# One list schedule for the layer norm, projections, short convolutions and preparation of a hybrid DeltaNet and mixture-of-experts layer

## The chip, the cores and the metric

The kernel runs on one core of one Trainium2 chip. The metric is device time in microseconds (us), the median of several runs. The engines are TensorE (PE, matrix products), VectorE (DVE), ScalarE (ACT), GpSimd (POOL) and SyncE (SP), whose queue issues most of the transfers (DMA).

## What is computed

One layer over 1024 latent tokens and 256 context tokens, width 1024. One input projection feeds a gated DeltaNet of four heads and a Conformer convolution; their outputs go through one output projection, and a mixture of 64 experts follows. The changed stage computes the parts in this excerpt that stand before the chunked scan: the Conformer's layer norm, the projections, the 7-tap convolutions, norms and decays, and the triangular matrix of each chunk with the inverse of its 16x16 diagonal blocks.

```python
u = modulate(rmsnorm(x, g_mix), sh1, sc1) @ w_in           # the same for ctx; columns: q k v | z | ba | cf
qkv = silu(depthwise_conv_seq(qkv, conv_w))                # 7 taps, ctx and x are separate sequences
q, k = l2norm(q) * DN_DK ** -0.5, l2norm(k)
beta, g = sigmoid(ba[0]), -exp(a_log) * softplus(ba[1] + dt_bias)
gc = cumsum(g)                                             # inside a chunk
decay = exp(gc[:, None] - gc[None, :])
lmat = strict_lower((k * beta) @ k.T * decay)
tinv = triangular_solve(eye + lmat, eye)                   # then the scan over the chunks
y = silu(layernorm(dwconv(cf[:512] * sigmoid(cf[512:])) + dw_b, ln_g, ln_b))
x = x + gt1 * (concat(gated_head_norm(o, z), y) @ w_out)
x = x + gt2 * moe_ffn(modulate(rmsnorm(x, g_ffn), sh2, sc2))
return rmsnorm(x, g_final)
```

## The kernel before

Feature maps lie with channels on the partitions and tokens along the row. `hTh` and `hTl` are the high and low part of the modulated input, 1280 tokens (256 of context first). A projection block is 128 output columns: `load_w` (L302 to L305) loads the weights in two halves into `wst`, ACT copies the high part `whi`, and POOL subtracts for the low part `wlo` (`split`, L293 and L294); `fm` (L320) makes three products for each of 8 slices of the depth (`hTh` and `hTl` by `whi`, `hTh` by `wlo`), for a context segment of 256 columns and two latent segments of 512.

The stage begins behind the Conformer's 31 taps on DVE (L427). Its pieces:

- the layer norm of `ycv`, two halves of 512 tokens: channel mean on PE (L462, L466), subtraction, squares, variance, `Sqrt`, reciprocal, `Silu`, store to `hc_d` (L462 to L488);
- twelve `qkv_block`s, four each for k, v and q: projection, copy into `cx` (latent) and `cc` (context) with zero edges, `conv7` (first tap on ACT, six on DVE, L548), `Silu` (L569). Blocks of k and v are then transposed on PE (L573), scaled and stored to `kv_d`; `key_norms` follows the k blocks;
- four `z_block`s: projection, `Silu`, store;
- `prep1` for five pairs of chunks (L694 to L717): the factors `rr` (L694), the key products (L698), the running sums of `gg` (L701, products of `rr` and a triangle), their `Exp` in `dm` (L703), factors `nb` (L706, L707), and the matrix `wt` (L708), which is stored to `wt_d`. Its diagonal blocks are gathered into `bounce` (L714) and spread over all partitions into `rep`, 1 MB (L717);
- `base_inverse` for each pair: 15 elimination steps on DVE (`tm` L730, `xf` L731), which read `rep`;
- `conv_out` for two column halves, eight row tiles each: the Conformer's part of the output projection from `hc_d` and the residual `x` (`hx`, L602 to L614);
- the query norms (`sqq` L766, L767, L772) and their scale `ssq` (L775). Then the next stage begins on DVE with `yy` (L846).

In this stage the program text gives the work piece by piece, and an automatic scheduler sets the order on each engine; `first()` puts the splits at high priority. From L793 on (`manual_schedule`) the order is written out: the class `Order` takes operations, each with an engine, a duration, the keys that it reads and writes, and a latency (0.2 unless given) before its result can be used, simulates them, and emits them by the longest path that is left. The later stages (inverses, scan, routing, experts) are such lists.

Of the kernel before, what the change touches and what calls it, by code (L numbers as in the profile page):

```python
# [149 lines left out]
def hybrid_kernel(tc, a, out):  # L150
# [318 lines left out]
    for hf in range(2):
        sl = slice(hf * 512, (hf + 1) * 512)  # L470
        pm = channel_mean(lambda j: ycv[:, j, sl])
        for j in range(4):
            V.tensor_sub(ycv[:, j, sl], ycv[:, j, sl], pm)

        def square(j):
            sq = lnp.tile([128, 512], F32, name="sql", bufs=2)
            S.activation(sq, ycv[:, j, sl], AF.Square)
            return sq

        pv = channel_mean(square)  # L480
        rv = lnp.tile([128, 512], F32, name="rv", bufs=1)
        V.tensor_scalar(rv, pv, EPS, None, op0=OP.add)
        S.activation(rv, rv, AF.Sqrt)
        V.reciprocal(rv, rv)
        for j in range(4):
            V.tensor_mul(ycv[:, j, sl], ycv[:, j, sl], rv)
            S.activation(ycv[:, j, sl], ycv[:, j, sl], AF.Silu, scale=vcol('ln_g', j), bias=vcol('ln_b', j))
            SY.dma_start(hc_d[:, j, sl], ycv[:, j, sl])  # L488
# [11 lines left out]
    def sct(name):  # L500
        return keep.tile([128, 2, 10, 4], F32, name=name)

    beta, gg = sct("beta"), sct("gg")
    tmp = lnp.tile([128, 2, 10, 4], F32, name="tmp")
    S.activation(beta, bav[:, 0], AF.Sigmoid)

    def per_dh(t):
        return t.rearrange("p (d h) -> p d h", d=2)[:, :, None, :].to_broadcast([128, 2, 10, 4])

    V.tensor_tensor(gg, bav[:, 1], per_dh(alb[:, 1]), op=OP.add)  # L510
    S.activation(tmp, gg, AF.Abs)
    S.activation(tmp, tmp, AF.Exp, scale=-1.0)
    S.activation(alb[:, 0], alb[:, 0], AF.Exp)
# [36 lines left out]
    def qkv_block(blk):  # L550
# [1304 lines left out]
```

## Time and profile before

| what | value |
|---|---|
| median of 3 runs | 1735.74 us (1734.1 to 1737.79) |
| the profiled execution | 1735.59 us, span 1733.9 us |
| mean granted clock of PE over the span | 0.968 |
| PE busy in the span | 1593.5 us (92%) |
| DVE | 992.9 us (57%) |
| ACT | 494.5 us (29%) |
| POOL | 534.4 us (31%) |

"Busy" is the time in which an engine runs an instruction; the share is of the whole span, in which the experts' products fill the second half. The changed stage lies between about 212 and 563 us. "Granted clock" is the share of full speed that PE was allowed; the two levels are 2.4 GHz (1.00) and 1.2 GHz (0.50). In the rows, `<-` behind a tile names what it is made from, and behind an idle time what ended it.

### The profile page before, as it was taken

What the parts mean: (1) busy time and instruction counts of PE and PEld (TensorE: products, weight loads), DVE (VectorE), ACT (ScalarE), POOL (GpSimd) and SP (SyncE); (2) the same over time, 40 slices, a digit from 0 to 9 for tenths busy, and PEclk for the clock granted to TensorE, in tenths of its full rate; (3) what the DMA queues carried; (4) which work ended last, traced back from release to release, by engine and by line L of the source; (5) the groups of instructions that cost most, each with busy time, mean ns of one, the idle gap of its engine ahead of it and who ended that gap; (6) DMA issues with size and microseconds to landing.
All of it is one profiled execution on the core that took longest, in us unless ns stands there. A gap on an engine that the chain in (4) does not pass through costs nothing. (4 is left out here: it accounts for less than half of the span.)

```text
span 1733.9 us, 23484 instructions
## 1 busy us (share of the span) xinstructions
PE 1593.5 (92%) x8380; PEld 933.8 (54%) x8380; DVE 992.9 (57%) x2236; ACT 494.5 (29%) x1072; POOL 534.4 (31%) x487
## 2 busy tenths in 40 slices
PE   5989999877759999798999999999999999999995
PEld 1557667765537899787544433444444344443442
DVE  2588988889671886877712443434344434343424
ACT  4541266634122212444212121212121211111212
POOL 1321214543212777832011232323232323232310
PEclk9999999997979999899999999999999999999997
DMA  9455123444643334766358999999999999999957
GB/s 312 160 174 178 38 65 95 111 113 123 169 141 123 121 104 150 242 217 219 119 218 305 338 335 332 314 364 314 323 383 361 329 330 322 324 385 347 353 131 246
DMA packets 151114, 404.35 MB, mean 233 GB/s; under 512 B 21175, under 2 KB 68692, under 8 KB 125396
## 3 DMA queue, kind: packets, MB, share of 16 engines
q1 hardware_dynamic: 131146, 338.82, 53.9%
q0 software_dynamic: 18288, 59.26, 14.5%
q10 hardware_dynamic: 1562, 4.76, 0.7%
q8 instruction: 67, 1.10, 0.3%
q14 instruction: 51, 0.42, 0.1%
HBM read 339.48 MB, written 71.43 MB: 237 GB/s over the span
## 5 line engine op out<-in xcount | busy, mean ns | idle before, releaser
L1353 PE MATMUL gu<-wg,hg 128*32 128x512 f32 (+2 forms) x1968 | 463.2, 599 | 0.6 <-issue 0.6
L1632 DVE SCALAR_TENSOR_TENSOR ob<-dn,wc,gt2b 128x512 f32<-128x512 f32 x124 | 93.1, 750 | 366.0 <-PE dn L1373 366.0
L1641 POOL DMA_INDIRECT acc<-ob,ic x89 | 134.6, 1512 | 527.5 <-DVE st L1563 467.1
L1353 PEld LDWEIGHTS gu<-wg,hg 128*32 128x32 f32 (+2 forms) x1968 | 148.4, 137 | 203.1 <-issue 159.2
L1373 PE MATMUL dn<-wd,sg 128*32 128x512 f32 (+2 forms) x984 | 226.8, 597 | 0.5 <-ACT sg L1364 0.5
L1607 ACT ACTIVATE hg<-xt,mf 128x128 f32<-128x128 f32 x248 | 93.4, 456 | 376.0 <-PE xt L1601 376.0
L320 PE MATMUL a<-hTh,whi 128*128 128x512 f32 (+1 forms) x448 | 172.0, 384 | 5.2 <-ACT cx L557 2.8
L320 PE MATMUL a<-hTl,whi 128*128 128x512 f32 (+1 forms) x448 | 170.3, 380 | 0.0
L320 PE MATMUL a<-hTh,wlo 128*128 128x512 f32 (+1 forms) x448 | 169.5, 378 | 0.0
L1373 PEld LDWEIGHTS dn<-wd,sg 128*32 128x32 f32 (+2 forms) x984 | 77.8, 137 | 143.5 <-issue 142.7
L294 POOL TENSOR_TENSOR wlo<-wst,whi 128x512 fp32r<-128x512 f32 x56 | 82.5, 1489 | 220.5 <-ACT whi L293 220.3
L1605 DVE TENSOR_SCALAR hg<-xt,mf 128x128 f32<-128x128 f32 x248 | 84.4, 402 | 50.8 <-PE xt L1601 50.8
L427 DVE SCALAR_TENSOR_TENSOR ycv<-yg,cfw,ycv 128x64 f32<-128x64 f32 (+14 forms) x120 | 101.3, 844 | 6.1 <-ACT ycv L421 2.9
L320 PEld LDWEIGHTS a<-hTh,whi 128*128 128x128 f32 x448 | 85.1, 190 | 32.4 <-issue 13.3
L1591 POOL DMA_INDIRECT xg<-xn_d,ig x62 | 76.7, 1237 | 63.9 <-issue 20.6
L320 PEld LDWEIGHTS a<-hTh,wlo 128*128 128x128 f32 x448 | 85.0, 190 | 18.4 <-issue 3.4
L320 PEld LDWEIGHTS a<-hTl,whi 128*128 128x128 f32 x448 | 85.1, 190 | 17.8 <-issue 3.0
L1552 DVE TENSOR_TENSOR oh<-posl 128x1024 bf16<-128x1024 f32 (+3 forms) x89 | 77.6, 897 | 0.0
L1601 PE MATMUL xt<-ident,xg 128*128 128x128 f32 x496 | 70.3, 285 | 0.0
L293 ACT ACTIVATE whi<-wst 128x512 fp32r<-128x512 f32 x56 | 33.0, 624 | 111.3 <-PE a L320 65.5
L1358 DVE TENSOR_TENSOR sg<-sg,gu 128x256 f32<-128x256 f32 x62 | 26.1, 421 | 63.7 <-ACT sg L1357 63.7
L1357 ACT ACTIVATE sg<-gu 128x256 f32<-128x256 f32 x62 | 23.8, 384 | 135.2 <-PE gu L1353 135.2
(444 smaller groups left out, 2503.7 us busy)
## 6 DMA issues: line engine op xcount, KB each, us to landing
wg<-exp_w_gate SPq DMA_DIRECT2D x64, 1024.0 KB
wg<-exp_w_up SPq DMA_DIRECT2D x64, 1024.0 KB
wd<-exp_w_down SPq DMA_DIRECT2D x64, 1024.0 KB
wm<-w_mod SPq DMA_DIRECT2D x24, 1024.0 KB
wst<-w_in SPq DMA_DIRECT2D x48, 256.0 KB
kv<-kv_d SPq DMA_DIRECT2D x20, 512.0 KB
rep<-bounce SPq DMA_DIRECT2D x5, 1024.0 KB
eb<-egr_d SPq DMA_DIRECT2D x18, 256.0 KB
```

What stands on the lines that cost most here:

```text
L294: eng.tensor_tensor(lo, st, hi.bitcast(F32), op=OP.subtract)
L320: PE.matmul(ps[:, :n], l[:, k, :], r[:, k, t0:t0 + n], start=(k == 0 and i == 0), stop=(k == 7 and i == 2))
L427: V.scalar_tensor_tensor(yc[:, lo:hi], yg[:, lo + d:hi + d], cfw[:, t * 4 + j:t * 4 + j + 1], yc[:, lo:hi], op0=OP.mult, op1=OP.add)
L1353: PE.matmul(pgu[o:o + n, :].rearrange("p (a f) -> p a f", a=2), lhsT(k, o, n), wts[r][0][:, :, k, :], start=(k == 0), stop=(k == 7), tile_ ...
L1373: PE.matmul(pd[o:o + n, :], aT[:, k, o:o + n], wts[r][1][:, k, hf * 512:(hf + 1) * 512], start=(k == 0), stop=(k == 1), tile_position=(0, ...
L1552: V.tensor_tensor(oh[:, :, o:o + n], N.iol[:, None, p0:p0 + n].to_broadcast([128, 8, n]), N.posr[:, :, r:r + 1].to_broadcast([128, 8, n]), ...
L1591: G.indirect_dma_start(out=xg, out_offset=None, in_=xn_d, in_offset=bass.IndirectOffsetOnAxis(ap=ig, axis=0), bounds_check=1023, oob_is_er ...
L1601: PE.transpose(pt[:, csl(q)], nth(B['xg'][:, 0:1024], 4 * j + q, 8), ident)
L1605: V.tensor_scalar(hg[:, k, :], pt[:, csl(q)], sc_[:, k:k + 1], sh_[:, k:k + 1], op0=OP.mult, op1=OP.add)
L1607: S.activation(hg[:, k, :], pt[:, csl(q)], AF.Identity, scale=sc_[:, k:k + 1], bias=sh_[:, k:k + 1])
L1632: V.scalar_tensor_tensor(ob[:, hs_], res[hf], B['wc'], N.gt2b[:, hs_], op0=OP.mult, op1=OP.mult)
L1641: G.indirect_dma_start(out=acc_d[turn[0]], out_offset=bass.IndirectOffsetOnAxis(ap=ic[:n], axis=0), in_=B['ob'][o:o + n], in_offset=None, ...
```

## The change

The whole stage is listed with `Order` and emitted as one list, under `manual_schedule`, which now begins ahead of it, as do the eight PSUM banks `bk` of the later stages. Helpers `TE`, `DVE`, `ACT`, `POOL` and `DMA` add an operation with its duration. The list's lengths are, for example, 2.76 us for half of a 512-column projection segment, 1.7 for a tap over 1283 columns, 0.62 for a high part, 1.35 for a low part, 0.8 for most transfers, and 3.0 with a latency of 4.0 for the spread. A second `Order()` follows for the later stages. With the listing go these edits:

- `kf` and the k and v blocks have 1283 columns: context, three zeros, latent. One `conv7` pass of 1283 replaces two (1024 and 256); `ksl(c)` finds a chunk. The zero edges of `cx` are cleared once.
- `prep1` makes two fp32 factors `rr`, both on POOL, and two fp32 products with `Ls` and `Us` (L869 of the changed kernel), in place of four rounded factors (two on POOL, two on DVE) and four products; the casts `LUr` and `ghl` go.
- The low part of `conv_out`'s `hcr` is always POOL's; it alternated between DVE and POOL.
- After the k blocks there is a third pair of weight tiles; the k blocks have two more output tiles and a second `sq` in `qf`; the spread goes into two halves of `qf` in turn (`rep_of`), in place of a tile `rep`.
- All `z` blocks stand with the v blocks, and `conv_out(0)` ahead of the second half of the q blocks in the list's text.

```diff
-    def conv7(dst, src, blk, n):
-        for t in range(7):
-            wt = cnv[:, t * 12 + blk:t * 12 + blk + 1]
-            if t == 0:
-                S.activation(dst, src[:, 0:n], AF.Copy, scale=wt)
-            else:
-                V.scalar_tensor_tensor(dst, src[:, t:t + n], wt, dst, op0=OP.mult, op1=OP.add)
...
-        for ci, c in enumerate(pair):
-            wt = prp.tile([128, 4, 128], F32, name="wt", bufs=1)
-            rr_ = [prp.tile([128, 4, 128], F32R, name="rr", tag=t, bufs=1) for t in ("rf", "rl", "rb")]
-            rr_.append(cvp.tile([128, 4, 128], F32R, name="rr", tag="sq", bufs=1))
-            for i, t in enumerate(rr_):
-                (G, V, G, V)[i].tensor_tensor(t, bm((Ui, Li)[i // 2]), b3(ghl[i % 2][:, i // 2, c].bitcast(F32)), op=OP.mult)
-            yield
-            kk = bank("b")
-            for h in range(4):
-                PE.matmul(kk[:, csl(h)], kf[:, h, csl(c)], kf[:, h, csl(c)], start=True, stop=True)
-            sg = bank("b")
-            for i, t in enumerate(rr_):
-                PE.matmul(sg, LUr[i // 2], flat(t), start=(i == 0), stop=(i == 3))
-            dm = prp.tile([128, 4, 128], F32, name="dm", bufs=1)
-            S.activation(flat(dm), sg, AF.Exp)
-            nb = prp.tile([128, 4, 128], F32, name="nb", bufs=1)
-            for h in range(4):
-                S.activation(nb[:, h], Ui, AF.Identity, scale=nbd[:, c, h:h + 1], bias=nb2b[:, c, h:h + 1])
-            G.tensor_tensor(nb, nb, dm, op=OP.mult)
-            V.tensor_mul(wt, h4(kk), nb)
...
-        rep = prp.tile([128, 2048], F32, name="rep", bufs=1)
-        SY.dma_start(rep, bass.AP(tensor=bounce.tensor, offset=bounce.offset, ap=[[2048, 8], [0, 16], [1, 2048]]))
...
-    prp = st_cv.enter_context(tc.tile_pool(name="prep", bufs=1, reuse_waits="tile"))
-    key_norms()
-    for h in range(4):
-        run_together([prep1(pairs[h])])
-        qkv_block(8 + h)
-        run_together([base_inverse(pairs[h])])
-    for h in range(3):
-        qkv_block(h)
-        if h == 0:
-            run_together([prep1(pairs[4])])
-        if h == 1:
-            run_together([base_inverse(pairs[4])])
-    run_together([conv_out(0)])
-    qkv_block(3)
-    z_block(0)
-    run_together([conv_out(1)])
-    for h in (1, 2):
...
+    def o_load_w(src, k=8, by=None):
+        j = turn_of("w", N.wbufs)
+        hi, lo = (lambda sl, t=t: t[j].rearrange("p (k n) -> p k n", k=k)[:, sl] for t in (WH, WL))
+        keys = []
+        open_ = ["prep"] if j == 2 else []
+        for i in range(0, k, k // 2):
+            s = turn_of("ws", 3)
+            sl, st, ks_ = slice(i, i + k // 2), WS[s].rearrange("p (k n) -> p k n", k=k // 2), f"ws{s}"
+            kh_, kl_ = f"wh{j}{2 * i // k}", f"wl{j}{2 * i // k}"
+            DMA(0.75, lambda st=st, sl=sl: SY.dma_start(st, src[:, sl, :]), w=[ks_])
+            if by is not None:
+                DVE(0.8, lambda st=st: V.tensor_tensor(st, st, by()[:, None, :].to_broadcast([128, k // 2, 1024 // k]),
+                                                       op=OP.mult), r=["rr3"], w=[ks_])
+            ACT(0.62, lambda st=st, sl=sl: S.activation(hi(sl), st, AF.Copy), r=[ks_, *open_], w=[kh_])
+            POOL(1.35, lambda st=st, sl=sl: G.tensor_tensor(lo(sl), st, hi(sl).bitcast(F32), op=OP.subtract),
+                 r=[ks_, kh_], w=[kl_])
+            keys += [kh_, kl_]
+        return hi, lo, keys
...
+        open_ = ["prep"] if kind == 2 else []
+        ACT(1.4, lambda: tap(0), r=[kc, *open_], w=[kd])
+        for t in range(1, 7):
+            DVE(1.7, lambda t=t: tap(t), r=[kc], w=[kd])
...
+            ACT(0.63, lambda hs=hs, parts=parts: S.activation(parts()[0], hs, AF.Copy), r=[ko], w=[ka])
+            POOL(1.35, lambda hs=hs, parts=parts: G.tensor_tensor(parts()[1], hs, parts()[0].bitcast(F32),
+                                                                  op=OP.subtract), r=[ko], w=[ka])
...
+    def rep_of(n):
+
+        h = 0 if n % 2 else 2
+        return qf[:, h:h + 2, :].rearrange("p a t -> p (a t)"), [f"qf{h}", f"qf{h + 1}"]
+
+    def o_prep1(n):
+        bounce = dp.tile([8, 16, 2, 4, 16], F32, name="bounce", bufs=3)
+        for ci, c in enumerate(pairs[n]):
+            krr = [f"rr{2 * ci + i}" for i in range(2)]
+            for i in range(2):
+                POOL(1.5, lambda i=i, c=c, ci=ci: G.tensor_tensor(
+                    N.RR[2 * ci + i], bm((Ui, Li)[i]), b3(gg[:, i, c]), op=OP.mult), r=["gg", "prep"], w=[krr[i]])
+            b, kb = bbank()
+
+            def products(b=b, c=c):
+                for h in range(4):
+                    PE.matmul(b[:, csl(h)], kf[:, h, ksl(c)], kf[:, h, ksl(c)], start=True, stop=True)
+
+            TE(0.95, products, r=[f"kf{h}" for h in range(4)], w=[kb])
+            b2_, kb2 = bbank()
+
+            def running(b=b2_, ci=ci):
+                for i in range(2):
+                    PE.matmul(b, (Ls, Us)[i], flat(N.RR[2 * ci + i]), start=(i == 0), stop=(i == 1))
+
+            TE(1.8, running, r=krr, w=[kb2])
+            ACT(0.6, lambda b=b2_: S.activation(flat(N.DM), b, AF.Exp), r=[kb2, "prep"], w=["dm"])
+
+            def factors(c=c):
+                for h in range(4):
+                    S.activation(N.NB[:, h], Ui, AF.Identity, scale=nbd[:, c, h:h + 1], bias=nb2b[:, c, h:h + 1])
+
+            ACT(1.9, factors, r=["b2", "prep"], w=["nb"])
+            POOL(1.35, lambda: G.tensor_tensor(N.NB, N.NB, N.DM, op=OP.mult), r=["dm"], w=["nb"])
+            DVE(0.7, lambda b=b: V.tensor_mul(N.WT, h4(b), N.NB), r=[kb, "nb"], w=["wt"])
+            DMA(0.8, lambda c=c: SY.dma_start(wt_d[c], N.WT), r=["wt"], w=[f"wtd{c}"])
+            if c >= 2:
+                DMA(0.8, lambda c=c: SY.dma_start(dm_d[c - 2], N.DM), r=["dm"])
+
+            def gather(ci=ci, c=c):
+                src = wt_d[c]
+                SY.dma_start(bounce[:, :, ci], bass.AP(tensor=src.tensor, offset=src.offset,
+                                                       ap=[[16 * 512 + 16, 8], [512, 16], [128, 4], [1, 16]]))
+
+            DMA(1.0, gather, r=[f"wtd{c}"], w=[f"bn{n}{ci}"])
+
+        def spread():
+            SY.dma_start(rep_of(n)[0], bass.AP(tensor=bounce.tensor, offset=bounce.offset,
+                                               ap=[[2048, 8], [0, 16], [1, 2048]]))
+
+        O("DMA", 3.0, spread, [f"bn{n}0", f"bn{n}1", "prep"], rep_of(n)[1], 0, 4.0)
...
+    def o_base_inverse(n):
+        kr = rep_of(n)[1]
+
+        def steps(m0, m1):
+            rep, xf = rep_of(n)[0], N.xf
+            if m0 == 0:
+                V.tensor_copy(xf.rearrange("p d u c -> p (d u) c"), Ic[:, None, :].to_broadcast([128, 16, 16]))
+            for m in range(m0, m1):
+                k = 15 - m
+                tm = N.tm[m % 2]
+                tgt = view(xf, m + 1, [[128 - (m + 1), 2], [16, 8], [1, k]])
+                src = view(xf, m, [[128 + 15 - 2 * m, 2], [16, 8], [0, k]])
+                wr = view(rep, m * 128 + m + 1, [[(15 - 2 * m) * 128 - (m + 1), 2], [16, 8], [1, k]])
+                V.tensor_tensor(tm[:, :, :, :k], src, wr, op=OP.mult)
+                V.tensor_tensor(tgt, tgt, tm[:, :, :, :k], op=OP.add)
+
+        for m0 in range(0, 15, 3):
+            DVE(2.3, lambda m0=m0: steps(m0, m0 + 3), r=[*kr, "ic"], w=["xf"])
...
+    POOL(0.6, pads, w=["cx0", "cx1"])
+    for hf in range(2):
+        o_norm_half(hf)
+    o_scalars()
+    for h in range(4):
+        o_qkv(4 + h)
+    o_masks()
+    once(open_prep, w=["prep", "rv", "sql0", "sql1", "gs", "egr", *(f"y{j}{hf}" for j in range(4) for hf in range(2))])
+    N.wbufs, turns["w"], turns["ot"] = 3, -1, 0
+    o_key_norms()
+    for h in range(4):
+        o_prep1(h)
+        o_qkv(8 + h)
+        o_z(h)
+        o_base_inverse(h)
+    o_qkv(0)
+    o_prep1(4)
+    o_qkv(1)
+    once(open_out, w=["ac0", "ac1"])
+    o_conv_out(0)
+    o_base_inverse(4)
+    o_qkv(2)
+    o_qkv(3)
+    o_conv_out(1)
+    o_query_norms()
+    O.emit()
```

PE at the start of the stage: `ycv` is the Conformer's result, `gtc` and `ms` belong to the stage before, and the rows `a<-hTh,whi` and so on are projections. Before:

```order
L320 MATMUL a<-hTl,whi 128x512
L320 MATMUL a<-hTh,wlo 128x512
L320 MATMUL a<-hTh,whi 128x512
L438 MATMUL b<-ident,gtc 32x128
L462 MATMUL b<-ycv,ones 32x512 x3
L320 MATMUL a<-hTl,whi 128x512
L320 MATMUL a<-hTh,wlo 128x512
```

Now (`bk_...` are the banks, `rv` the copied mean, L670 the projections):

```order
L256 MATMUL a<-wm,csil 32x512 x7
L265 MATMUL b<-ident,ms 128x128 x4
L438 MATMUL b<-ident,gtc 32x128
L524 MATMUL bk_1381<-ycv,ones 32x512 x4
L528 MATMUL bk_1382<-rv,onm 128x512
L524 MATMUL bk_1381<-ycv,ones 32x512 x3
L670 MATMUL bk_1378<-hTh,whi 128x512
L670 MATMUL bk_1378<-hTl,whi 128x512
```

Before, projections stand ahead of and behind the first products with `ycv`; now these products and the mean's L528 stand ahead of all projections.

DVE at the first base inverse: `ac` are a v block's taps, `wt` is a chunk's matrix, `tm<-xf,rep` the first reader of the spread. Before:

```order
L548 SCALAR_TENSOR_TENSOR ac<-cx,cnv,ac 128x1024
L548 SCALAR_TENSOR_TENSOR ac<-cc,cnv,ac 128x256
L708 TENSOR_TENSOR wt<-b,nb 128x512
L548 SCALAR_TENSOR_TENSOR ac<-cc,cnv,ac 128x256
L694 TENSOR_TENSOR rr<-Ui,gg_1537 128x512
L548 SCALAR_TENSOR_TENSOR ac<-cc,cnv,ac 128x256
L694 TENSOR_TENSOR rr<-Li,gg_1537 128x512
L548 SCALAR_TENSOR_TENSOR ac<-cc,cnv,ac 128x256
L548 SCALAR_TENSOR_TENSOR ac<-cx,cnv,ac 128x1024
L730 TENSOR_TENSOR tm<-xf,rep 128x16x15
```

Now (L719 the taps, L745 the scaling of a transposed v block, L880 `wt`, L913 and L914 the steps; the spread lies in `qf`):

```order
L745 TENSOR_TENSOR ot_1406<-bk_1381,rk 128x256
L719 SCALAR_TENSOR_TENSOR ac_2047<-cx_1404,cnv,ac_2047 128x1283 x6
L906 COPY xf<-Ic 128x256
L913 TENSOR_TENSOR tm_2057<-xf,qf 128x16x15
L914 TENSOR_TENSOR xf<-xf,tm_2057 128x2x8x15
L913 TENSOR_TENSOR tm_2058<-xf,qf 128x16x14
L914 TENSOR_TENSOR xf<-xf,tm_2058 128x2x8x14
L913 TENSOR_TENSOR tm_2057<-xf,qf 128x16x13
L914 TENSOR_TENSOR xf<-xf,tm_2057 128x2x8x13
L880 TENSOR_TENSOR wt<-bk_1382,nb 128x512
```

All six taps of the second v block stand ahead of the first reader of the spread, in one run, and the third `wt` stands behind it and three steps.

DVE at the second base inverse, before:

```order
L548 SCALAR_TENSOR_TENSOR ac<-cx,cnv,ac 128x1024
L736 TENSOR_TENSOR yc<-yc,Ic 128x128
L723 COPY xf<-Ic 128x256
L548 SCALAR_TENSOR_TENSOR ac<-cx,cnv,ac 128x1024
L548 SCALAR_TENSOR_TENSOR ac<-cc,cnv,ac 128x256
L694 TENSOR_TENSOR rr<-Ui,gg_1537 128x512
L730 TENSOR_TENSOR tm<-xf,rep 128x16x15
L548 SCALAR_TENSOR_TENSOR ac<-cc,cnv,ac 128x256
L731 TENSOR_TENSOR xf<-xf,tm 128x2x8x15
L708 TENSOR_TENSOR wt<-b,nb 128x512
```

Now:

```order
L745 TENSOR_TENSOR ot_1405<-bk_1384,rk 128x256
L719 SCALAR_TENSOR_TENSOR ac_2046<-cx_1403,cnv,ac_2046 128x1283 x2
L906 COPY xf<-Ic 128x256
L913 TENSOR_TENSOR tm_2057<-xf,qf 128x16x15
L914 TENSOR_TENSOR xf<-xf,tm_2057 128x2x8x15
L913 TENSOR_TENSOR tm_2058<-xf,qf 128x16x14
L914 TENSOR_TENSOR xf<-xf,tm_2058 128x2x8x14
L913 TENSOR_TENSOR tm_2057<-xf,qf 128x16x13
L914 TENSOR_TENSOR xf<-xf,tm_2057 128x2x8x13
L719 SCALAR_TENSOR_TENSOR ac_2046<-cx_1403,cnv,ac_2046 128x1283
```

Two of the six taps of the third v block stand ahead of the reader of the spread, and the next one behind three steps.

## Rows read from the trace of the kernel before

**Rows 1.** Windows: us; busy (x count) of PE, PEld, DVE, ACT, POOL; PEclk; DMA.

```profile
187.00:212.00 25.00, 23.50 (x125) 17.44 (x123) 24.00 (x34) 2.24 (x4) 6.29 (x16) 1.00 0.13 32
212.00:563.00 351.00, 290.26 (x1292) 220.58 (x1293) 259.70 (x429) 153.09 (x245) 109.44 (x105) 0.91 0.41 116
```

**Rows 2.** Timeline of PE at the start of the stage.

```profile
212.19 1.04 PE L462 MATMUL b<-ycv,ones 128*32 128x512 f32 x2 [1.70 <-DVE ycv L427]
```

**Rows 3.** Timeline of DVE at the end of the stage.

```profile
562.09 0.17 DVE L773 COPY ssq<-b 128x16 f32<-128x16 f32 x1 [6.13 <-PE b L772]
563.25 1.29 DVE L846 TENSOR_TENSOR yy<-yc,bd 128x512 f32<-128x512 f32 x2
```

**Rows 4.** Waits of 212 to 563: us in total, times, longest.

```profile
DVE tm L730 <- DMA rep<-bounce: 23.6, 5, 9.5
DVE hx L613 <- DMA hx<-x: 16.4, 4, 5.1
```

**Rows 5.** Timeline of SP's DMA queue and of DVE: start, us.

```profile
326.42 0.64 SPq L717 DMA_DIRECT2D rep<-bounce  x1
338.40 0.41 DVE L730 TENSOR_TENSOR tm<-xf,rep 128x240 f32<-128x240 f32 x1 [1.25 <-DMA rep<-bounce]
428.54 0.60 SPq L717 DMA_DIRECT2D rep<-bounce  x1
442.01 0.41 DVE L730 TENSOR_TENSOR tm<-xf,rep 128x240 f32<-128x240 f32 x1 [4.09 <-DMA rep<-bounce]
```

**Rows 6.** Timeline of PE, two pieces: start, us, records.

```profile
285.48 0.40 PE L320 MATMUL a<-hTh,whi 128*128 128x512 f32 x1
289.57 0.39 PE L320 MATMUL a<-hTh,whi 128*128 128x512 f32 x1
557.80 1.04 PE L767 MATMUL b<-sqq,ones 128*32 128x512 f32 x2
558.78 0.50 PE L320 MATMUL a<-hTl,whi 128*128 128x512 f32 x1
```

**Rows 7.** PE's groups by form, 212 to 572: busy us, mean ns, idle before.

```profile
L320 PE MATMUL a<-hTh,whi 128*128 128x512 f32 x232 | 93.0, 401 | 5.2 <-ACT cx L557 2.8 <-DVE hx L613 2.4
L612 PE MATMUL a<-whi,hcr 128*128 128x512 f32 x128 | 47.6, 448 | 11.0 <-ACT whi L293 6.2 <-DVE hcr L294 3.3 <-POOL hcr L294 0.8
L612 PE MATMUL a<-wlo,hcr 128*128 128x512 f32 x64 | 28.1, 439 | 1.0 <-POOL wlo L294 1.0
L701 PE MATMUL b<-rr,lu 128*128 128x512 f32 x40 | 13.6, 435 | 4.1 <-DVE ot L582 2.5 <-DVE rr L694 1.1 <-POOL rr L694 0.4
```

**Rows 8.** Timeline of PE after two of its gaps.

```profile
281.98 2.39 PE L573 MATMUL b<-ident,kf 128*128 128x128 f32 x10 [3.03 <-ACT kf L569]
504.16 2.44 PE L767 MATMUL b<-sqq,ones 128*32 128x512 f32 x4 [17.63 <-ACT sqq L766]
```

**Rows 9.** Windows after these gaps, columns as in rows 1.

```profile
282.00:284.00 2.00, 2.00 (x10) 2.00 (x11) 2.00 (x4) 1.84 (x3) 0.00 (x0) 0.50 0.00 0
284.00:286.00 2.00, 2.00 (x13) 1.91 (x12) 2.00 (x4) 1.15 (x3) 0.00 (x0) 0.76 0.60 176
504.00:507.00 3.00, 2.64 (x5) 0.55 (x6) 2.02 (x7) 1.51 (x4) 0.00 (x0) 0.50 0.28 78
507.00:510.00 3.00, 3.00 (x7) 0.90 (x5) 2.50 (x8) 1.51 (x4) 0.00 (x0) 0.50 0.18 52
```

**Rows 10.** Timeline of SP's queue, first and last store of a conv_out.

```profile
513.65 0.34 SPq L614 DMA_DIRECT2D yo_d<-hx  x1
539.15 0.34 SPq L614 DMA_DIRECT2D yo_d<-hx  x1
```

**Rows 11.** DVE's groups of 212 to 563 for the running sums' factors.

```profile
L694 DVE TENSOR_TENSOR rr<-Ui,gg 128x512 fp32r<-128x512 f32 x10 | 10.4, 1044 | 1.6 <-PE b L701 1.6
L694 DVE TENSOR_TENSOR rr<-Li,gg 128x512 fp32r<-128x512 f32 x10 | 9.0, 899 | 0.0
```

**Rows 12.** ACT's groups of 212 to 563, table loads of one line.

```profile
L703 ACT ACT_TABLE_LOAD x5 | 6.4, 1283 | 0.1
```

More of the change, by code (lines that the diff above doesn't have):

```diff
@@ L469, in hybrid_kernel @@
[L469 to L488, printed above, removed]
@@ L500, in sct @@
[L500 to L513, printed above, removed]
@@ L533, in hybrid_kernel, with ksl @@
-    SY.dma_start(egr_d, egr)
-    st_l.close()
+    kf = keep2.tile([128, 4, 1283], F32, name="kf")
+    def ksl(c):
+        return slice(c * 128 + 3 * (c > 1), c * 128 + 3 * (c > 1) + 128)
     st_g = ExitStack()
@@ new lines, in o_key_norms, with factors @@
+    def o_key_norms():
+        DVE(0.2, lambda: V.tensor_scalar(ssk, ssk, EPS, None, op0=OP.add),
+            w=["rk", *(f"ssk{h}{i}" for h in range(4) for i in (0, 4, 8))])
+        ACT(0.3, lambda: S.activation(rk, ssk, AF.Sqrt), w=["rk"])
+        def factors():
+            V.reciprocal(irk, ssk)
+            V.tensor_tensor(b2, beta, irk[:, None].to_broadcast([128, 2, 10, 4]), op=OP.mult)
+            V.tensor_scalar(nb2b, b2[:, 1], -1.0, None, op0=OP.mult)
+            V.tensor_sub(nbd, b2[:, 1], b2[:, 0])
+            V.tensor_mul(bS, b2, eg[:, 1])
+        DVE(1.3, factors, r=["rk", "beta", "eg"], w=["b2"])
@@ new lines, in hybrid_kernel, with last @@
+    YCT = [gbase.tile([128, 8, 16], F32, name=f"yc{n}") for n in range(5)]
+    def o_base_inverse(n):
[14 more added lines that the diff above has]
+            DVE(2.3, lambda m0=m0: steps(m0, m0 + 3), r=[*kr, "ic"], w=["xf"])
+        def last():
+            yc = YCT[n]
+            V.tensor_add(yc, N.xf[:, 0], N.xf[:, 1])
+            V.tensor_tensor(yc, yc, Ic[:, None, :].to_broadcast([128, 8, 16]), op=OP.subtract)
+        DVE(0.9, last, r=["xf"], w=[f"yc{n}"])
+        for ci, c in enumerate(pairs[n]):
+            YC[c] = YCT[n][:, 4 * ci:4 * ci + 4, :]
@@ new lines, in hybrid_kernel @@
+    o_qkv(0)
[9 more added lines that the diff above has]
+    O.emit()
+    st_cv.close()
+    st_w.close()
+    st_d = ExitStack()
+    gq = st_d.enter_context(tc.tile_pool(name="gq", bufs=1, side="right", reuse_waits="tile"))
+    st_gp = ExitStack()
+    gp = st_gp.enter_context(tc.tile_pool(name="gd", bufs=1, side="right", reuse_waits="tile"))
+    st_i = ExitStack()
@@ L809, in tile4 @@
+    ip = st_i.enter_context(tc.tile_pool(name="inv", bufs=1, reuse_waits="tile"))
+    O = Order()
     def tile4(pool, name, tag=None):
```

508 lines of the change are left out of this document (291 added, 217 removed).

## Prediction

> **What bounds the kernel now.** I read the windows of the trace first, to see which engine fills the changed stage, then TensorE's (PE's) groups, then the waits, then single stretches of the timeline.
>
> The stage starts when VectorE (DVE) ends the conformer's taps: the layer norm's first product waits for them and starts at 212.19 [rows 2]. It ends when the query scale `ssq` is done and the next stage's first product `yy` starts on DVE at 563.25 [rows 3]. That is 351 us, and what follows is not touched, so I pass a shift of this end on at its full size. In these 351 us PE is busy 290.3 us, DVE 259.7, ACT 153.1, POOL 109.4, and PE's granted clock is 0.91 on the mean [rows 1]. PE is the nearest to a bound, but it is not one: it idles 61 us, and 0.09 x 351 = 32 us of full clock are lost beside that. Also to be seen in [rows 1]: PE was busy 23.5 of the 25 us before 212, with projections that were taken ahead of the taps' end.
>
> The waits name a culprit for a part of the idle time: DVE waits 23.6 us, in five pieces, for the 1 MB spread `rep<-bounce` [rows 4]. The spread's own length is in [rows 5]: issued at 326.42, its reader starts at 338.40, 11.98 us later; in the longest of the five, 428.54 to 442.01, 13.47. I take the middle, 12.7.
>
> **PE's work in the changed stage.** A product of 512 columns takes 0.227 us, from 18 of them between 285.48 and 289.57 [rows 6]. The projections have 768 of these (32 half blocks with 8 x 3 products each; the trace has 232 of each of the three kinds after 212 [rows 7], the others lie before it): 174.5 us. The 192 of 256 columns at half as much make 22 us. The 192 of `conv_out` (L612, 128 and 64 in [rows 7]) make 43.6. The running sums change from four rounded products for a chunk to two in fp32: an fp32 product (two records) takes 0.98 us, 557.80 to 558.78 [rows 6], so 20 of them take 19.6, where 40 took 13.6 of busy time [rows 7]; at 0.227 they are worth 9.1, so the edit adds 10.5 us to PE. The rest, counted alike: layer norm 12, key products 9, transposes 9, query norms 7.5, scalars 1.5. Together 299, say 300.
>
> A second way gives the same: 23.5 + 290.3 + 8 (the last projections run on behind 563) less 32 for the clock is 290 of work before, and 10 more makes 300.
>
> **What the list moves.** First, a loss. The order on PE puts every projection behind the layer norm's first products, which wait for the taps, so the 23.5 us done ahead now stand behind 212.2. PE will have idled some 23 us by then. After the 17.6 us gap at 504 the clock stayed at 0.50 for the next 6 us [rows 8, 9], which is 3 us lost; I add this 3, and 0.8 for the first weight split, which stands behind the channel mean's copy on ACT: 3.8 (bounds 0.8 and 6).
>
> Second, the gain: PE's other idle time. By its listed lengths the planner keeps PE nearly fed, with `z` projections between the `v` blocks, a third pair of weight tiles, and extra output tiles in `qf`. If nothing were late the stage would end at 212.2 + 3.8 + 300 + 1.2 (last transposes to `yy`, 562.09 to 563.25 [rows 3]) = 517.2, 46 us earlier.
>
> Third, what the list has too short. The spread is listed with 3.0 us and a latency of 4.0, 7.0 in all; the trace has 12.7 [rows 5], so each comes 5.7 us later than planned. DVE takes its instructions in order, and the rows shown in the change put the reader of the spread ahead of work that PE needs: ahead of the third `wt` (whose bank and tile the next `prep1` needs) in the first base inverse, and ahead of four of the six taps of a `v` block in the second. The four spreads of the `v` blocks stand so. Before, the same rows mixed taps and `wt` in between, but also behind the reader. I pass the full 5.7 on four times: 22.8 us (bounds 0, if PE's listed lead and its `z` projections cover them, and 5 x 5.7 = 28.5, if the fifth, ahead of `conv_out`'s adds, passes on too). I take a value near the upper end, since PE's list is tight and the delays stand one behind the other, and the waits of before did pass on in part: the gaps behind them are on PE too.
>
> Each stall of PE over some 3 us also took clock: after the 3.03 us gap that ends at 281.98 the clock was 0.50 and then 0.76 for 2 us each [rows 8, 9], (0.50 + 0.24) x 2 = 1.5 us. Four times: 6 us (bounds 0 and 12, two such for each).
>
> The second `conv_out` has no `z` projections left beside it. Before, its eight stores ran from 513.65 to 539.15, 25.5 us for seven steps [rows 10], 3.64 a tile where PE's part is 12 x 0.227 = 2.73; PE filled the rest with projections. The row buffers `hx` are two as before, and DVE waited 16.4 us for them [rows 4]. So 8 x 0.91 = 7.3 us come into the open (bounds 0 and 14.6, for both halves).
>
> **What I cost at nothing.** DVE loses 19.4 us of `rr` [rows 11] and 5 of the `conv_out` split: DVE has 91 us to spare, so nothing comes of it unless a wait hides there. The conv taps in one pass of 1283 columns in place of two: the dependent passes of 1024 and 256 interleave, so a pass saves only its fixed part, and DVE has room. The split on POOL alone: POOL is idle two thirds of the stage; uncovered it would cost 8 x 0.6 us. Gap columns in `kf`, pads cleared once: under 1 us.
>
> **The sum.** 212.2 + 3.8 + 300 + 22.8 + 6 + 7.3 + 1.2 = 553.3, against 563.25: 10 us earlier. From the profiled execution, 1735.59 us (the median of the runs is 1735.74), this gives 1725.6.
>
> The Trainium skill has another price for the spread: "DMA: Bandwidth & Descriptors", section "Anatomy of one DMA — SWDGE (gpsimd) path", fits a transfer as 2.0 us and its bytes over 436 GB/s. For 1 MB that is an estimate of 4.4 us, on another queue kind than here. By it the spread would be in time and the sum would be without 22.8 and 6: 1697. The trace, 12.0 to 13.5 [rows 5], disagrees, and the measurement decides.
>
> **The rivals.**
> *The lateness is covered.* PE has a `z` block for each `v` block, 48 x 0.227 = 11 us, to run while DVE waits, and the waits of before show on PE only in part. Then 22.8 and 6 fall away: 1697, and without the 7.3 as well 1689.5. Against it: DVE's order, in which the reader of the spread stands first. 20%.
>
> *Nothing left.* The lateness also meets the fifth spread and clock costs double: 5.7 + 6 more eat the 10, so 1732 to 1739. 13%.
>
> *ACT is the new wait (slower).* The planner's lengths for ACT hold no table loads. One takes 1283 ns [rows 12]. In the order of the changed kernel ACT has 28 in this stage, where before has 18, and 25 of the 28 stand in no listed length: 25 x 1.283 = 32 us. ACT splits every weight block, copies every projection out of its bank, and each load sits right ahead of such work. If all were passed on to PE: 1757.7; half: 1741.6. The point that decides is 10 us, that is 8 of the 25; over 13.5 us, 11 of them, the kernel is measurably slower. For it: ACT's order is now fixed by the list, and Silu, Exp, Sqrt alternate more. Against it: ACT is busy 153 of 351 us [rows 1], and the loads of before have 0.1 us of idle time ahead of them [rows 12], with none of it seen on PE. 27%.
>
> The Trainium skill's "ScalarE: Activation LUTs", section "What ACT_TABLE_LOAD costs", counts 1283 ns and a drain of some 1380 beside it. By that estimate the 25 are worth 66 us, and a sixth of them would undo the gain. The trace agrees on the load; a drain has no row of its own here.
>
> **How the numbers follow.** The forecast holds 40% for itself, with its own range 1713 to 1732 (a spread more or less covered, clock 0 to 12). With the rivals: 20% end at 1689 to 1713, 13% at 1732 to 1739, 27% above. The range 1696 to 1748 leaves out some half of the first rival and the worst third of the last. Faster by over 0.2% (3.5 us, about what a measurement of this kernel can tell from no change): 0.60; within: 0.13; slower: 0.27.
>
> **What would show it.** Right: no projection on PE between 190 and 212 and a busy PE from 216; five waits of DVE for the spread, each over 3 us, with PE gaps behind four of them; a granted clock of about 0.95 in the stage; first `yy` near 553. Wrong: a PE without gaps between 216 and 517 (first rival); gaps on PE that end with an ACT copy or split behind a table load (last rival); or a loss in the stages behind, which I hold to be unchanged.

## The result, and the profile after

The changed kernel takes 1745.15 us (median of 5 runs, 1743.39 to 1747.05), the kernel before 1735.74 (5 runs): ratio 1.0055, 95% interval 1.0041 to 1.007. It is 9.4 us slower, and the forecast was 10 us faster.

All of it lies in the changed stage. DVE's timeline at its end, against [rows 3]:

```profile
572.77 0.17 DVE L947 COPY ssq<-bk 128x16 f32<-128x16 f32 x1 [2.35 <-PE bk L944]
574.07 1.28 DVE L1038 TENSOR_TENSOR yy<-yc,bd 128x512 f32<-128x512 f32 x2
```

The first `yy` stands at 574.07 where it stood at 563.25, 10.8 us later; the span grew by 9.2 (1733.9 to 1743.1), so what follows is 1.6 us shorter. The windows of the changed kernel, columns as in [rows 1]:

```profile
187.00:212.00 25.00, 5.91 (x32) 1.67 (x31) 23.25 (x39) 1.12 (x3) 6.22 (x12) 0.64 0.01 1
212.00:220.00 8.00, 7.31 (x19) 2.33 (x18) 5.84 (x25) 4.37 (x9) 4.04 (x4) 0.64 0.26 66
530.00:560.00 30.00, 30.00 (x125) 22.45 (x123) 22.21 (x18) 12.47 (x19) 9.84 (x7) 1.00 0.40 127
212.00:574.00 362.00, 319.27 (x1421) 239.71 (x1419) 248.42 (x352) 171.63 (x261) 121.18 (x86) 0.94 0.43 119
```

PE is idle for 43 of the 362 us, where it was for 61 of 351, and its mean granted clock is 0.94 where it was 0.91. That mean is over the whole stretch, with PE's gaps in it. The stage keeps PE better fed, as the list means to, and still ends later. The head start is gone: 5.9 us of PE in the 25 before 212, against 23.5. PE's larger gaps, from its timeline:

```profile
211.70 1.91 PE L524 MATMUL bk<-ycv,ones 128*32 128x512 f32 x2 [16.45 <-DVE ycv L427]
360.86 0.85 PE L736 MATMUL bk<-ident,ac 128*128 128x128 f32 x4 [3.86 <-DVE wt L880]
408.37 2.39 PE L736 MATMUL bk<-ident,ac 128*128 128x128 f32 x10 [6.04 <-ACT ac L725]
457.31 2.40 PE L736 MATMUL bk<-ident,ac 128*128 128x128 f32 x10 [12.85 <-ACT ac L725]
482.28 0.50 PE L786 MATMUL bk<-whi,hcr 128*128 128x512 f32 x1 [3.41 <-POOL hcr L777]
488.39 0.79 PE L786 MATMUL bk<-wlo,hcr 128*128 128x512 f32 x1 [3.52 <-POOL wlo L657]
503.21 0.50 PE L786 MATMUL bk<-whi,hcr 128*128 128x512 f32 x1 [2.93 <-ACT hcr L776]
```

Three of them, 3.86, 6.04 and 12.85, stand behind DVE's reader of the spread: the third `wt` behind the first, the taps `ac` of the third and fourth v block behind the others. The same reader on DVE's timeline, against [rows 5]:

```profile
357.43 0.66 DVE L913 TENSOR_TENSOR tm<-xf,qf 128x240 f32<-128x240 f32 x1 [4.22 <-DMA qf<-bounce]
390.98 0.41 DVE L913 TENSOR_TENSOR tm<-xf,qf 128x240 f32<-128x240 f32 x1 [8.24 <-DMA qf<-bounce]
431.96 0.41 DVE L913 TENSOR_TENSOR tm<-xf,qf 128x240 f32<-128x240 f32 x1 [12.76 <-DMA qf<-bounce]
```

The issues of the first and the third of these spreads on SP's queue:

```profile
345.00 0.64 SPq L893 DMA_DIRECT2D qf<-bounce  x1
419.54 0.62 SPq L893 DMA_DIRECT2D qf<-bounce  x1
```

345.00 to 357.43 is 12.4 us and 419.54 to 431.96 again 12.4. The five spreads lie between 11.9 and 14.3 from issue to reader. From the waits of 187 to 600 us (us in total, times, longest), the two lines that answer to [rows 4]:

```profile
DVE tm L913 <- DMA qf<-bounce: 29.1, 5, 12.8
DVE rr L792 <- DMA rr<-x: 9.8, 4, 4.1
```

The reader waits 29.1 us, more than the 23.6 of before. `rr` L792 is the row of `x` that `hx` held before. Windows at and behind PE's larger gaps (columns as in [rows 1]) show how much of the low clock met work:

```profile
361.18:364.60 3.42, 3.42 (x16) 3.13 (x14) 3.25 (x9) 3.19 (x6) 0.12 (x1) 0.50 0.19 77
408.37:412.38 4.01, 4.01 (x15) 3.62 (x16) 3.84 (x8) 2.52 (x6) 2.51 (x2) 0.50 0.38 120
444.47:457.31 12.84, 0.00 (x0) 0.00 (x0) 10.32 (x23) 2.31 (x2) 0.00 (x0) 0.58 0.25 54
457.31:460.17 2.86, 2.86 (x11) 2.53 (x12) 2.31 (x8) 0.94 (x1) 0.00 (x0) 0.50 0.02 4
488.39:494.30 5.91, 5.91 (x14) 4.46 (x14) 5.91 (x5) 1.58 (x2) 3.14 (x2) 0.50 0.92 151
503.21:508.00 4.79, 3.93 (x9) 2.94 (x10) 4.58 (x9) 0.63 (x1) 2.55 (x2) 0.64 0.71 209
```

In the gap of 12.85 the clock fell, but PE had nothing to do there: only the 2.86 us behind it cost time, 1.4 us. The trace's clock records, laid over PE's busy records, give 12.4 us of clock lost to work in the whole stage and 7.6 in gaps. PE's work at full clock is so 319 - 12.4 = 307 us.

ACT's groups from 187 to 575, against [rows 12]:

```profile
L872 ACT ACT_TABLE_LOAD x9 | 11.5, 1283 | 7.5 <-issue 4.1 <-DVE ot L745 2.0 <-PE bk L869 1.3
L756 ACT ACT_TABLE_LOAD x6 | 7.7, 1283 | 5.8 <-DMA kv_d<-ot 5.7
```

The Exp of the decays (L872) loads its table 9 times where it was 5, and z's Silu (L756) 6 times, as both alternate.

### The profile page after: what moved, and what is told of

Read it like the earlier page. It is cut to its first block, busy times and chain, and to the rows that moved or that the text cites. A ratio compares the mean times of both kernels' runs of the same rounds, so it can differ in the third digit from the quotient of the medians.

```text
span 1743.1 us, 23352 instructions
## 1 busy us (share of the span) xinstructions
PE 1601.1 (92%) x8380; PEld 934.8 (54%) x8380; DVE 975.8 (56%) x2156; ACT 500.3 (29%) x1070; POOL 538.9 (31%) x461
## 3 DMA queue, kind: packets, MB, share of 16 engines
q0 software_dynamic: 18288, 59.26, 14.3%
## 5 line engine op out<-in xcount | busy, mean ns | idle before, releaser
L670 PE MATMUL bk<-hTh,whi 128*128 128x512 f32 (+1 forms) x320 | 124.4, 389 | 4.1 <-ACT ot L756 2.6
L670 PE MATMUL bk<-hTl,whi 128*128 128x512 f32 (+1 forms) x320 | 118.8, 371 | 0.0
L670 PE MATMUL bk<-hTh,wlo 128*128 128x512 f32 (+1 forms) x320 | 118.7, 371 | 0.0
L427 DVE SCALAR_TENSOR_TENSOR ycv<-yg,cfw,ycv 128x64 f32<-128x64 f32 (+14 forms) x120 | 97.6, 813 | 6.6 <-ACT ycv L421 3.3
L657 POOL TENSOR_TENSOR wlo<-wst,whi 128x512 fp32r<-128x512 f32 x40 | 60.2, 1518 | 107.4 <-ACT whi L656 107.3
L670 PEld LDWEIGHTS bk<-hTh,whi 128*128 128x128 f32 x320 | 60.9, 190 | 26.6 <-issue 5.6
L670 PEld LDWEIGHTS bk<-hTl,whi 128*128 128x128 f32 x320 | 60.9, 190 | 11.0 <-issue 1.4
L670 PEld LDWEIGHTS bk<-hTh,wlo 128*128 128x128 f32 x320 | 60.6, 189 | 10.9
L1793 PEld LDWEIGHTS xt<-ident,xg 128*128 128x128 f32 x496 | 60.3, 194 | 1.4 <-issue 1.4
```

The source lines that it names most:

```text
L427: V.scalar_tensor_tensor(yc[:, lo:hi], yg[:, lo + d:hi + d], cfw[:, t * 4 + j:t * 4 + j + 1], yc[:, lo:hi], op0=OP.mult, op1=OP.add)
L657: POOL(1.35, lambda st=st, sl=sl: G.tensor_tensor(lo(sl), st, hi(sl).bitcast(F32), op=OP.subtract), r=[ks_, kh_], w=[kl_])
L670: PE.matmul(b[:, :n], l(k), r[:, k, t0:t0 + n], start=(k == 0 and i == 0), stop=(k == 7 and i == 2))
L1793: PE.transpose(pt[:, csl(q)], nth(B['xg'][:, 0:1024], 4 * j + q, 8), ident)
```

## The experiments

Theory when they began: the stage is PE's work, 300 us from 212 on, plus what the late spread adds. First rival: ACT's table loads. Second: waits on a chain of several engines set the time, and PE's work is hidden in them. "The first `yy`" is the end of the stage; the changed kernel has it at 574.07. Three of the kernels leave part of the computation out; the routing and so the experts' time change with that, and for them only the stage is read. A ratio is to runs of the kernel before that were taken beside the kernel (medians 1735.2 to 1736.2 us). A first `yy` is read from one profiled execution, and the runs of one kernel differ by some 5 us (1718.93 to 1724.43 in the first experiment), so differences of a few us at the first `yy` are not told from nothing.

**The spread's latency in the list.**

```diff
-        O("DMA", 3.0, spread, [f"bn{n}0", f"bn{n}1", "prep"], rep_of(n)[1], 0, 4.0)
+        O("DMA", 3.0, spread, [f"bn{n}0", f"bn{n}1", "prep"], rep_of(n)[1], 0, 10.0)
```

> The changed kernel with one number changed: the list's latency for the 1 MB spread is 10.0 in place of 4.0, so 13.0 in all, near the 11.9 to 14.3 us of the trace. Theory (the stage is PE's work, and the stalls behind DVE's reader of the spread come on top): the three PE gaps of 3.9, 6.0 and 12.9 us shrink to under 10 together, with less time at the low clock, and the kernel is 15 to 30 us faster than the changed one, so 1715 to 1730 us. Rival (the gaps come from ACT's table loads or other waits, the spread is only the last to arrive): less than 5 us gained, above 1740 us.

Measured: 1722.03 us, ratio to before 0.992 (0.9901 to 0.9939). One number turns the loss of 9.4 us into a gain of 14. Its end on DVE's timeline:

```profile
552.73 1.29 DVE L1038 TENSOR_TENSOR yy<-yc,bd 128x512 f32<-128x512 f32 x2
```

The whole stage in a window, columns as in [rows 1]:

```profile
212.00:552.70 340.70, 318.02 (x1421) 238.55 (x1419) 257.63 (x350) 168.76 (x259) 124.65 (x86) 0.96 0.45 126
```

The largest gap of PE that is left, from its timeline:

```profile
418.90 0.79 PE L670 MATMUL bk<-hTh,whi 128*128 128x512 f32 x1 [4.66 <-ACT ot L756]
```

DVE no longer waits for the spread at all (no such line among its waits), PE is idle for 22.7 us in place of 43, 4.66 at most at a time, and the stage is 21.3 us shorter.

The forecast has a number for this case too: without its 22.8 for the spread and 6 for the clock its sum ends at 524.5, and the measured end is 552.73, 28 us later. The order is another one, but what the forecast had wrong is in the rest of its sum, not in the spread.

**The head start, alone and with the latency.** The entry stands for the taps in the list and emits nothing; the second kernel has both edits and also keeps the zero edges and masks of GpSimd behind it.

```diff
+    O("TAPS", 23.0, lambda: None, (), [f"y{j}{hf}" for j in range(4) for hf in range(2)])
     for hf in range(2):
         o_norm_half(hf)
```

> The changed kernel with one entry more in the list: an entry of 23 us on an engine of its own, which writes the layer norm's input, so the list knows that the Conformer's taps end some 23 us after PE is free; it emits nothing. Theory (the head start of 23.5 us of projections was lost and is on PE's path): projections stand before the layer norm again, PE is busy for most of 190 to 212 us, and the kernel is 18 to 26 us faster than the changed one, so 1719 to 1727 us. Rival (the time is set by the stalls behind, which keep their places on DVE and ACT): under 8 us gained.

> The changed kernel with both entries: the spread's latency of 13.0 in all, and an entry of 23 us ahead of the layer norm; the clearing of the zero edges and the masks on GpSimd also wait for this entry, so that they no longer stand ahead of the low parts (they held the first low part until 203 us in the run with the entry alone). Theory (once the spread is planned in time, PE's work sets the stage, so work done ahead of 212 us counts): PE busy for 17 us or more of 190 to 212, the first yy near 535 us, 1700 to 1710 us. Rival (other chains set the time, as the 4.4 us of the run with the entry alone suggest): no better than the run with the spread's latency, 1717 us or above.

Measured: 1740.72 us alone (ratio 1.0023, 1.0007 to 1.0038), first `yy` at 573.57; with the latency 1728.69 (0.995, 0.9932 to 0.9968), first `yy` at 555.65. The window before 212 of the kernel with the entry alone:

```profile
187.00:212.00 25.00, 11.98 (x59) 7.17 (x52) 22.72 (x30) 1.87 (x3) 12.16 (x15) 0.73 0.13 32
```

The same window with both edits:

```profile
187.00:212.00 25.00, 18.70 (x107) 14.64 (x107) 23.22 (x38) 1.02 (x3) 0.00 (x0) 1.00 0.02 3
```

With both, PE works 18.7 us ahead, four fifths of what it did before the change, and the stage ends 2.9 us later than with the latency alone. This is against the theory: the work that PE did early did not make the stage end earlier. The entry alone gained 4.4 us of the 18 to 26 expected, the size of the rival. The order changes with the entry, so how much of the head start this new order costs elsewhere was not separated.

**One fp32 product less.** The running sums without the product with `Us`; the first kernel lists the rest with 0.9 us and so gets another order, the second keeps 1.8 us and the order of the run with the latency.

```diff
-                for i in range(2):
-                    PE.matmul(b, (Ls, Us)[i], flat(N.RR[2 * ci + i]), start=(i == 0), stop=(i == 1))
+                PE.matmul(b, Ls, flat(N.RR[2 * ci]), start=True, stop=True)
```

> The changed kernel without the second of the two fp32 products of the running sums (the backward direction's is left out, so its decays are not computed); the list has 0.9 us for the remaining one. PE's work falls by 10 products of 0.98 us, 9.8 us. Theory (PE's work is on the path of the whole stage): 7 to 10 us faster than the changed kernel, about 1736 us. Rival (waits set the time and PE's work is hidden in them): under 3 us.

> The run with the spread's latency of 13.0, without the second fp32 product of the running sums (the backward direction's decays are left out), but with the list's length of 1.8 us kept, so that every engine's order is word for word the one of that run and PE alone has 9.8 us less to do. The routing changes with the result, so only the stage counts: the first yy stood at 552.7 us. PE's work on the path of the stage: yy at 543 to 546. A chain of other engines sets the middle of the stage: yy at 549 to 553, and PE's idle time grows by what its work lost.

Measured, the stage alone: first `yy` at 575.30 in the one (574.07 with the product) and at 554.03 in the other (552.73 with it). The window of the second's stage:

```profile
212.00:554.00 342.00, 312.67 (x1401) 236.10 (x1401) 256.07 (x353) 168.56 (x259) 122.84 (x86) 0.95 0.44 125
```

PE's busy time falls by 5.4 us, at a mean clock of 0.95 where it was 0.96, its idle time grows from 22.7 to 29.3 us, and the end does not come a microsecond earlier (one run). In that order the products that were taken out are not on the path: where PE no longer works, it waits. That decides for the second rival in the order of the run with the latency and for these products, which stand there between some 320 and 442 us. In the changed kernel's own order this was not tested, as the first of the two kernels has another order.

**ACT's table loads.** First z's gate left out, then the loads put into the list beside the latency.

```diff
-            ACT(0.6, lambda b=b, o=o: S.activation(flat(OT[o]), b, AF.Silu), r=[kb], w=[f"ot{o}"])
+            ACT(0.6, lambda b=b, o=o: S.activation(flat(OT[o]), b, AF.Copy), r=[kb], w=[f"ot{o}"])
```

> The changed kernel with Copy in place of Silu behind the z projections (z's gate function is left out). Silu of z and Exp alternate on ACT in the changed kernel, so about 10 of the 28 table loads of the stage go, 13 us of ACT time. Rival (ACT's unlisted table loads hold PE up): 8 us or more faster than the changed kernel, under 1737 us. Theory (they are hidden): under 4 us.

```diff
-            ACT(0.6, lambda b=b, o=o: S.activation(flat(OT[o]), b, AF.Silu), r=[kb], w=[f"ot{o}"])
+            ACT(1.9, lambda b=b, o=o: S.activation(flat(OT[o]), b, AF.Silu), r=[kb], w=[f"ot{o}"])
...
-            ACT(0.6, lambda b=b2_: S.activation(flat(N.DM), b, AF.Exp), r=[kb2, "prep"], w=["dm"])
+            ACT(1.9, lambda b=b2_: S.activation(flat(N.DM), b, AF.Exp), r=[kb2, "prep"], w=["dm"])
```

> The run with the spread's latency of 13.0, and beside it the table loads listed where they come most often: 1.9 us in place of 0.6 for z's Silu and for the Exp of the decays. If ACT's unlisted loads hold the stage up: 5 us or more faster than with the latency alone, under 1717 us. If not: 1718 to 1727 us.

Measured: without the gate the stage has 19 loads in place of 28, and the first `yy` is at 570.49, 3.6 us earlier, under the 4 us that speak for "hidden"; DVE's wait for the spread fell beside it from 29.1 to 24.6 us. The other 19 loads were not taken out. With the loads listed 1740.07 us (1.0027, 1.0012 to 1.0041), a miss of both expectations: 18 us slower than with the latency alone. Its waits for the spread, from the waits of DVE:

```profile
DVE tm L913 <- DMA qf<-bounce: 2.9, 2, 1.5
```

Its end on DVE's timeline:

```profile
570.82 1.29 DVE L1038 TENSOR_TENSOR yy<-yc,bd 128x512 f32<-128x512 f32 x2
```

DVE hardly waits for the spread there, and the stage is only 3.2 us shorter than in the changed kernel. So a list that knows the spread's length is not enough. The order that came out has other gaps; PE's largest, from its timeline, stands behind a v block's Silu:

```profile
448.07 2.40 PE L736 MATMUL bk<-ident,ac 128*128 128x128 f32 x10 [8.23 <-ACT ac L725]
```

Why this order is worse was not settled.

**The spread as four transfers**, in the changed kernel, in the one before, and in the one with the latency.

```diff
-            SY.dma_start(rep_of(n)[0], bass.AP(tensor=bounce.tensor, offset=bounce.offset,
-                                               ap=[[2048, 8], [0, 16], [1, 2048]]))
+            for i in range(4):
+                SY.dma_start(rep_of(n)[0][:, i * 512:(i + 1) * 512],
+                             bass.AP(tensor=bounce.tensor, offset=bounce.offset + i * 512,
+                                     ap=[[2048, 8], [0, 16], [1, 512]]))
```

> The changed kernel with its list as it is, but the spread issued as four transfers of 512 columns each (2 KB packets in place of 8 KB, the same 1 MB). It tells whether the 12 to 14 us belong to the transfer's form, and tests the same step from the other side: not the plan is made longer, but the transfer shorter. If it lands in under 9 us: the PE gaps of 3.9, 6.0 and 12.9 us shrink and the kernel is 10 to 22 us faster than the changed one, 1723 to 1735 us. If the form does not matter: 12 us again and no change, 1742 to 1750 us.

> The kernel before with the same four transfers in place of one. DVE waited 23.6 us for the spread there, and some of PE's 60 us of gaps stand behind it. If the form shortens the transfer by 4 us or more: up to 10 us faster than before, 1726 to 1734 us. If it does not: 1734 to 1738 us.

> The run with the spread's latency of 13.0, with the spread issued as four transfers of 2 KB packets. The four gave the kernel before 10.6 us and the changed one 6.4. If the two ways to meet the late spread are the same time saved twice: within 3 us of 1722. If the shorter transfer still shortens the chain wt, spread, inverse: 1714 to 1719 us.

Measured: 1738.74 us in the changed kernel (1.0013, 1.0001 to 1.0025), 1725.3 in the one before (0.9936, 0.9917 to 0.9954), 1718.19 with the latency (0.9895, 0.9878 to 0.9911). The first is the test with the list's lengths untouched; every engine's order is that of the changed kernel. The three spreads that DVE waits for there take 10.3 to 11.8 us, not under 9, and the gain of 6.4 us lies between the two expectations. DVE's waits for the spread in it:

```profile
DVE tm L915 <- DMA qf<-bounce: 20.5, 3, 10.7
```

The end of its stage on DVE's timeline:

```profile
568.27 1.29 DVE L1040 TENSOR_TENSOR yy<-yc,bd 128x512 f32<-128x512 f32 x2
```

The wait falls by 8.6 us (from 29.1) and the stage by 5.8, so two thirds of it reach the end; if that rate held for all 29.1, they would be worth some 20 us, an estimate, about what the latency gave. The kernel before gained 10.6 us, though its spreads became only 1.0 to 3.8 us shorter, where 4 were expected to be needed. The last of the three kernels has the lowest median of the study, 1.05% under the kernel before and some 27 us under the changed one. It lies in the range of the second expectation, but its interval overlaps that of the latency alone, so a gain beside the latency is not shown.

**The fifth spread in a tile of its own.** Theory: the taps of the last two q blocks wait for the last base inverse, since the fifth spread lies in their halves of `qf`. The room comes from the third pair of weight tiles; the third kernel is the control.

```diff
-    N.wbufs, turns["w"], turns["ot"] = 3, -1, 0
+    N.wbufs, turns["w"], turns["ot"] = 2, -1, 0
...
+        if n == 4:
+            return N.rep, ["rep"]
         h = 0 if n % 2 else 2
```

> The changed kernel, its list's lengths as they are, but the fifth spread goes into a tile of its own in place of the halves of qf that belong to the third and fourth q block; the room comes from the third pair of weight tiles, so there are two. Theory (the end of the stage hangs on a chain: fifth wt, fifth spread, last base inverse, and only then the taps of the last two q blocks and the query norms): these taps run before or between the last base inverse, and the first yy is 8 to 20 us earlier, 1725 to 1737 us. Rival (PE's work ends the stage, the taps only wait in time): within 4 us of the changed kernel.

> The same with the spread's latency of 13.0 in the list. Theory: the two gains add up, 8 to 15 us faster than the run with the latency alone, 1707 to 1714 us, first yy near 540 us. Rival: no faster than the run with the latency alone, 1718 us or more.

> The control for the two others: the changed kernel with the spread's latency of 13.0 and two pairs of weight tiles, the fifth spread in qf as in the changed kernel. If the third pair is worth something beside the late spread: 1726 to 1735 us. If not: 1718 to 1725 us, and what the run with the own tile gains is the tile's.

Measured: 1747.44 us (1.0061, 1.0044 to 1.0078) with the listed lengths, 1730.18 (0.9961, 0.995 to 0.9973) with the latency, and the control 1729.9 (0.9962, 0.9948 to 0.9977). The own tile gives nothing; this theory falls. The third pair of weight tiles is worth 7 to 8 us (ratios 0.9962 and 0.992). And between the first two, which differ in the latency alone, it gives 17.3 us again.

## Why the prediction was wrong

By its steps, in its order.

- *The following stages pass the shift on.* Right: 10.8 us at the first `yy`, 9.2 in the span.
- *PE's work of 300 us from 212 on.* Somewhat too small: 307 were measured. The second way, which seemed to confirm 300, took all 32 us of lost clock off PE's busy time. Part of that loss fell in gaps, in which PE had no work (the row behind this list). With the 18 us that fell on work by the trace's records, the second way gives 304 for the kernel before.
- *The sum itself* is the step that failed as a mechanism. "PE's work in the changed stage" was taken as a base to which stalls are added, as if each microsecond of it moved the end. Taking 9.8 us of it away, in the order of the run with the latency, moved nothing (554.03 against 552.73). Work done ahead of 212 did not shorten the stage either, though there the order changed too.
- *Start 3.8.* Right in size: 0.7 idle and, between 212 and 220, 0.36 x 8 = 2.9 of clock.
- *If nothing were late, PE stays fed.* Wrong, a term put at nothing: gaps under 2 us outside `conv_out` make some 6 us in the changed kernel, and with the spread in time PE still idled 22.7 us.
- *The spread, 22.8.* Right in place; the size agrees in part by luck: four delays of 5.7 us were forecast, and 3.86 + 6.04 + 12.85 = 22.75 us of PE's gaps stand behind three readers. Three of DVE's five waits are over 3 us, where five were forecast. That the lateness costs about this much is shown by the shorter transfer in the same order, and by the latency (21.3 us) in another order.
- *Clock, 6 us.* Right in size for what it was meant for: behind the three gaps of the spread the low clock took 1.7 + 2.0 + 1.4 = 5.1 us from PE's work. That short gaps of `conv_out` would cost clock too, 4.6 us behind 488 and 503, was in no term.
- *`conv_out`, 7.3.* Mis-sized, and at another place. I had the last tiles wait for `hx`; there PE is full (530 to 560: 30.0 of 30). The gaps lie in the first half, 3.41 + 3.52 + 2.93 and two smaller ones of 0.9 and 1.5, 12 us in all, most of them behind ACT's and GpSimd's splits, while DVE's wait for `x` fell from 16.4 us [rows 4] to 9.8.
- *The end, 1.2.* Right: 572.77 to 574.07.

The largest gap of PE in the kernel before, columns as in [rows 1]; 0.41 x 17.63 = 7.2 us of its lost clock fall there on no work:

```profile
486.53:504.16 17.63, 0.00 (x2) 0.00 (x1) 12.72 (x18) 2.74 (x5) 2.61 (x2) 0.59 0.53 138
```

Added up along PE, the 20.8 us that the sum of 553.3 is short of 574.07 are about 7 of work, 6 of short gaps, and at `conv_out` 5 of idle time and near 5 of clock, less some 1.5 in the other terms. No part is large; together they decided the sign, as the forecast gain was 10. This is an account of where PE's time went and not of causes: the run without the products shows that a term taken out of it can come back as idle time.

Of the rivals none came as written. ACT's table loads gave the right side and nearly the right time, but the cause is not shown to be theirs: 28 loads came as counted, and nine fewer of them gave 3.6 us. "The lateness is covered" was wrong. None of them had what the runs show: with one length far too short the list gives an order that costs more than the automatic one, while PE's idle time falls; and with that length mended it still gains 14 us over the kernel before, where the sum without the spread's terms promised 39.

The Trainium skill's fit for a transfer ("DMA: Bandwidth & Descriptors", section "Anatomy of one DMA — SWDGE (gpsimd) path"), an estimate of 4.4 us for the spread, is not borne out by 12.4 in the changed kernel either.

What stays open: which chain of engines sets the end once the spread is in time, as no run names it; and why the list with the table loads is 18 us worse than that without, and so how much of the latency's 21 us is the wait itself and how much the luck of an order. For the wait speak the run with four transfers in the list as it was, and 17.3 us for the latency with two weight tiles.

## What to carry to other kernels

One listed length that is far too short can cost a list schedule more than it gains, though better lengths alone did not always give a better order here: compare each listed latency, of transfers above all, with the issue-to-use time of a trace, and look on in-order engines at what stands behind the reader of a late transfer. Busy PE is not the path: before adding PE's work and its stalls up, take some of the work out with the order kept and see whether the end moves. A mean clock over a stretch counts gaps in which the engine had no work, so read it where the engine is busy before taking it off the work. Orders that come out of nearly the same list can differ by 1%, so time several.

## What the runs showed of the hardware

The form of a transfer of the same 1 MB matters: the kernel before gained 10.6 us by it. As 128 packets of 8 KB it was used 12 to 13.5 us after its issue [rows 5]; as four transfers with packets of 2 KB, in the kernel before, the second spread stands so on SP's queue:

```profile
376.78 2.51 SPq L718 DMA_DIRECT2D rep<-bounce  x4
```

Its reader on DVE's timeline:

```profile
387.53 0.41 DVE L732 TENSOR_TENSOR tm<-xf,rep 128x240 f32<-128x240 f32 x1 [2.04 <-DMA rep<-bounce]
```

That is 10.75 us, though the four issues take 2.5 us of SP's time; the same spread took 12.8 before the edit (376.48 to 389.24). DVE's waits for the five fell from 23.6 us [rows 4] to 10.3 in that kernel:

```profile
DVE tm L732 <- DMA rep<-bounce: 10.3, 3, 7.9
```

The five came 9.4 to 12.0 us after their issue there, and the first `yy` of that kernel stands at 553.12, 10.1 us earlier. Why the smaller packets come sooner was not tested.
